# Last layer-0 down projection, its norm and the first value products, one stream after the other

## The chip, the cores and the metric

The kernel runs on one core of one Trainium2 chip. The metric is the device time of one execution in microseconds (us). TensorE (PE) multiplies matrices and loads its weights beside that (PEld); VectorE (DVE), ScalarE (ACT) and GpSimd (POOL) do the elementwise work; SyncE (SP) issues the loads.

## What is computed

Two layers of a backbone over two streams of 256 tokens with 2048 channels, latent (stream 0) and context (stream 1). Each layer is a mixer and a gated MLP, each behind an RMS norm with a shift and a scale that come from `c`. Layer 0 mixes by pooling, layer 1 by neighbourhood attention in which latent queries read the context keys and values too. In float32:

```
h  = h  + ml[:, 5] * conv_ffn(modulate(rms_norm(h,  norm2_g[0]), ...))    # latent, end of layer 0
hc = hc + mc[5]    * conv_ffn(modulate(rms_norm(hc, norm2_g[0]), ...))    # context
a_lat = modulate(rms_norm(h,  norm1_g[1]), ml[:, 0], ml[:, 1])            # start of layer 1
a_ctx = modulate(rms_norm(hc, norm1_g[1]), mc[0], mc[1])
q, k, v = a_lat @ w_qkv;  kc, vc = a_ctx @ w_qkv[:, D:]
def conv_ffn(u, ...): return (silu(conv3(u @ w_gate) + b) * (u @ w_up)) @ w_down    # 5504 hidden channels
def rms_norm(x, g):   return x * rsqrt(mean(x * x, channels) + 1e-6) * g
```

## The kernel before

Channels lie on the 128 partitions, so a stream is 16 tiles `h_of(s)[:, k, :]` of 128 x 256 (`hl` latent, `hc` context). Every float32 product is three products of split operands: a high half (rounded, float32r) and a low half (the rest), `hi*xh + hi*xl + lo*xh`. Weights are loaded from memory in pieces of up to 1024 columns into six staging rooms (`load`, `stage`); `split` makes the high half on ScalarE (line 143) and the low half on VectorE (line 145) in one of three `whp` buffers, or four while `extra` holds the pool `whx`.

The MLP's 43 hidden tiles are worked in chunks of four; the last chunk has three. `gate0` leaves a chunk's activations in `act` rooms (`act_tile`, seven of them) with both streams side by side, 512 columns. `down0` (lines 653 to 672) multiplies a chunk with its down weights: four groups `mg` of four output tiles, and for each output nine matmuls of 512 columns (three hidden tiles, lines 657 to 659) into a PSUM bank. In the last chunk VectorE adds the bank to `hl` and `hc` (line 663) and `n3.add` sums squares for the next norm: two squares on ScalarE (line 276), one add of 512 columns on VectorE (line 282). `pump` advances by one step what is left of layer 1's modulation at each call.

After the last output `n3.rstd()` works serially: matmuls of the square sums with ones (`n3s`, line 289), three small VectorE steps and a power on GpSimd (line 294), a diagonal (`n3d`, line 297), and a matmul that spreads the result over the partitions (`n3b`, line 299), left in PSUM. `normalise` (line 310 to 313) then makes, for each tile k and stream, y on VectorE, the high half of A on ScalarE and the low half on VectorE. y takes a `t2` tile, six of which exist. `_values` goes over four groups `kg` of four tiles k: it loads and splits a group of value weights, normalises the group for both streams, and does 48 matmuls of 512 columns into four banks `v_first` (two per stream; lines 869 to 871). The keys (`kq_tile`, line 934) come next.

Each engine works through its instructions in an order fixed before the run by a planner: it takes the earliest instruction in the program's text among those that it expects to be ready, and gives a tile any free buffer of its tag.

Of the kernel before, what the change touches and what calls it, by code (L numbers as in the profile page):

```python
# [10 lines left out]
F32 = mybir.dt.float32  # L11
F32R = mybir.dt.float32r
AF = mybir.ActivationFunctionType
ALU = mybir.AluOpType
# [3 lines left out]
P = 128  # L18
D = 2048
KT = D // P  # L20
T = 256
# [36 lines left out]
def kernel(ctx: ExitStack, tc: tile.TileContext, xT, cxT, wmod, wg, wu, wd, wp,  # L58
                         wq, wv, wo, vec, cc, rope, inv, strips, out):
    nc = tc.nc  # L60
# [94 lines left out]
    both = (0, 1)  # L155
# [105 lines left out]
    def M(l, which, k, s):  # L261
        return modT[l, which * 4 + k // 4][:, k % 4, s : s + 1]


    class Norm:


        def __init__(self, streams, pool, name):
            self.streams, self.pool, self.name = streams, pool, name
            self.n = T * len(streams)  # L270
            self.acc = None

        def add(self, h_of, k):
            sq = self.pool.tile([P, 512], F32, tag="t2", name=f"{self.name}q{k}")
            for s in self.streams:
                nc.scalar.activation(sq[:, T * s : T * s + T], h_of(s)[:, k, :], AF.Square)
            if k == KT - 1:
                self.last = sq
            elif self.acc is None:
                self.acc = sq  # L280
            else:
                nc.vector.tensor_tensor(self.acc[:, : self.n], self.acc[:, : self.n], sq[:, : self.n], op=ALU.add)

# [19 lines left out]

    def normalise(l, which, h_of, streams, rstd, pool, ks=range(KT), keep=A):

        for k in ks:
            a = ap0.tile([P, 2, 2, T], F32R, tag=f"A{k}", name=f"A{k}_{l}_{which}")
            y = pool.tile([P, 2, T], F32, tag="t2", name=f"nrm{l}{which}{k}")
            for s in streams:
                nc.vector.scalar_tensor_tensor(y[:, s], h_of(s)[:, k, :], M(l, which + 1, k, s),  # L310
                                               rstd[:, T * s : T * s + T], op0=ALU.mult, op1=ALU.mult)
# [4 lines left out]
            if l == 1 and k == 1:  # L316
                hold[:] = [ins.ins]
# [5 lines left out]
    with ExitStack() as ph0:  # L323
# [10 lines left out]
        def h_of(s):  # L334
            return hc if s else hl
# [50 lines left out]
        with ExitStack() as phs:  # L386
# [53 lines left out]
            def mixer(g):  # L440
# [3 lines left out]
                nc.sync.dma_start(inv_t, inv[:, g, :])  # L444
                gsc = st.tile([P, 8], F32, bufs=1, name=f"gsc{g}")
                gbi = st.tile([P, 8], F32, bufs=1, name=f"gbi{g}")
                pa = []
# [190 lines left out]

        n3 = Norm(both, f0, "n3")

        def down0(c, fs, acts, after=None):
            n = len(fs)
            last = c == len(chunks) - 1
            for mg in range(4):
# [4 lines left out]
                for m in range(4):  # L649
# [10 lines left out]
                    k = 4 * mg + m  # L660
                    if last:
                        for s in both:
                            nc.vector.scalar_tensor_tensor(h_of(s)[:, k, :], ps[:, T * s : T * s + T], M(0, 5, k, s),
                                                           h_of(s)[:, k, :], op0=ALU.mult, op1=ALU.add)
                        n3.add(h_of, k)
                    else:
                        y = f0.tile([P, 2, T], F32, tag="t2", name=f"dy{c}_{k}")
                        for s in both:
                            nc.scalar.activation(y[:, s], ps[:, T * s : T * s + T], AF.Copy, scale=M(0, 5, k, s))  # L669
                            nc.gpsimd.tensor_tensor(h_of(s)[:, k, :], h_of(s)[:, k, :], y[:, s], op=ALU.add)  # L670
                if after is not None:
                    after()

        r6 = late(NC)
# [24 lines left out]
        prev = (len(chunks) - 1, chunks[-1], [acts[f] for f in chunks[-1]])  # L699
        down0(*prev)  # L700
        for _ in pump:
            pass
        extra.clear()
        rooms.extend(-r for r in ring)

        rstd = n3.rstd()
        _values(bank, nc, ld, A, wv, 0, lambda ks: normalise(1, 0, h_of, both, rstd, f0, ks), v_first)
        hold.clear()

# [143 lines left out]

def _values(bank, nc, ld, A, wv, g, before, pv):

    pv.extend(bank("gu", f"v{g}_{i}") for i in range(4))
    for kg in range(4):
        parts = ld(wv[g, kg], f"wv{g}_{kg}")
        if before is not None:
            before(range(4 * kg, 4 * kg + 4))  # L860
        for i in range(4):
# [12 lines left out]
def _attention(tc, ap0, bank, ld, A, M, hl, wq, wv, wo, rope, strips, ident, v_first):  # L874
# [9 lines left out]
    with ExitStack() as es:  # L884
# [27 lines left out]
        def v_group(g):  # L912

            if g == 0:
                pv = v_first
            else:
                pv = []
                _values(bank, nc, ld, A, wv, g, None, pv)
# [293 lines left out]
```

## Time and profile before

| | us |
|---|---|
| median of 3 runs | 3107.48 |
| lowest and highest | 3105.3, 3110.52 |
| profiled execution | 3105.55 |
| its span, first to last instruction | 3103.8 |
| TensorE matmul busy | 3033.5 (98%) |
| VectorE, ScalarE, GpSimd busy | 1948.5, 1371.4, 820.2 |

The times are of whole executions; the profile is of one, and its rows count from the first instruction. A matmul's row gives when it starts and how long it takes through the array; matmuls overlap, so the distance between two starts is what one costs.

### The profile page before, as it was taken

Reading aid. Unit: us, or ns where it says so; the run is one execution under the profiler, and the core shown is the slowest. Engines: PE = TensorE matmul, PEld = TensorE weight load, DVE = VectorE, ACT = ScalarE, POOL = GpSimd, SP = SyncE. Lnnn points to the kernel's source line nnn. Section 1 sums busy time; section 2 is a strip of 40 time slices with the busy share of each in tenths; the row PEclk is TensorE's granted clock in tenths of the full one; section 3 lists DMA queues with packets and bytes.
Section 4 is the critical chain, followed back from the end, with each engine's and each line's share of the span. In section 5 each row is a group of like instructions: output and inputs, shape, how many; then the busy total and the mean of one; then the engine's idle time right before and its main releaser. Section 6 shows DMA issues by size and latency. Waiting matters only on the chain.

```text
span 3103.8 us, 40829 instructions
## 1 busy us (share of the span) xinstructions
PE 3033.5 (98%) x15082; PEld 2409.9 (78%) x15082; DVE 1948.5 (63%) x2748; ACT 1371.4 (44%) x2219; POOL 820.2 (26%) x823
## 2 busy tenths in 40 slices
PE   6999899999999999999999999999999999999998
PEld 2565558888888888888887787878778888888887
DVE  4445674384765748567485665474777677766676
ACT  4333455323233332333334444343545665656665
POOL 2011213213031130302213000000002466556665
PEclk9999999999999999999999999999999999999999
DMA  9888573274746648475573233332345565665563
GB/s 381 331 275 309 179 237 98 90 230 143 243 149 200 203 154 256 131 218 178 175 233 117 97 108 108 103 111 97 112 144 182 180 196 186 191 188 188 177 192 120
DMA packets 177927, 559.70 MB, mean 180 GB/s; under 512 B 17600, under 2 KB 22208, under 8 KB 177728
## 3 DMA queue, kind: packets, MB, share of 16 engines
q1 hardware_dynamic: 177728, 557.10, 55.6%
q8 instruction: 119, 1.95, 0.2%
q14 instruction: 80, 0.66, 0.1%
HBM read 554.93 MB, written 2.10 MB: 179 GB/s over the span
## 4 chain that ended last, share of the span: by engine, by line
PE 94%; DMA 2%; DVE 2%; POOL 1%; ACT 1%; issue 1%; SPq 0%; DVEq 0%; ACTq 0%; POOLq 0%
PE g L764 5%; PE u L764 5%; PE d L657 5%; PE d L659 5%; PE d L658 5%; PE d L809 4%; PE u L631 4%; PE u L632 4%; PE u L633 4%; PE g L631 4%; PE g L633 4%; PE g L632 4%; PE mod L193 3%; PE g L765 3%; PE u L765 3%; PE d L810 2%
## 5 line engine op out<-in xcount | busy, mean ns | idle before, releaser
L670 POOL TENSOR_TENSOR hl<-hl,dy 128x256 f32<-128x256 f32 x160 | 149.3, 933 | 957.9 <-ACT dy L669 956.6
L821 POOL TENSOR_TENSOR hl<-hl,dy 128x256 f32<-128x256 f32 x320 | 322.2, 1041 | 182.1 <-ACT dy L819 179.8
L241 DVE SCALAR_TENSOR_TENSOR macc<-wm,sc,macc 128x512 f32<-128x512 f32 (+1 forms) x360 | 325.0, 933 | 72.0 <-DMA wm<-wmod 71.2
L669 ACT ACTIVATE dy<-d,modT 128x256 f32<-128x256 f32 x320 | 133.4, 470 | 195.8 <-PE d L659 194.5
L193 PE MATMUL mod<-wm,sc 128*32 128x512 f32 x768 | 133.6, 619 | 23.7 <-DMA wm<-wmod 23.7
L670 POOL TENSOR_TENSOR hc<-hc,dy 128x256 f32<-128x256 f32 x160 | 127.0, 794 | 0.0
L145 DVE TENSOR_TENSOR wd_2l<-wd,wd_2h 128x1024 fp32r<-128x1024 f32 (+1 forms) x44 | 54.1, 1235 | 111.5 <-ACT wd_2h L143 111.5
L819 ACT ACTIVATE dy<-d,modT 128x512 f32<-128x512 f32 x160 | 104.5, 684 | 37.4 <-PE d L810 36.1
L908 POOL TENSOR_TENSOR rk<-rk,rp 128x256 f32<-128x256 f32 x16 | 13.8, 861 | 365.6 <-DVE rk L907 301.9
L145 DVE TENSOR_TENSOR wd_3l<-wd,wd_3h 128x1024 fp32r<-128x1024 f32 (+1 forms) x44 | 52.0, 1202 | 80.1 <-ACT wd_3h L143 80.1
L145 DVE TENSOR_TENSOR wd_1l<-wd,wd_1h 128x1024 fp32r<-128x1024 f32 (+1 forms) x44 | 53.5, 1221 | 58.4 <-ACT wd_1h L143 58.4
L466 POOL TENSOR_TENSOR pf<-ws,inv 128x256 f32<-128x256 f32 x32 | 27.7, 886 | 221.8 <-DVE ws L461 154.1
L193 PEld LDWEIGHTS mod<-wm,sc 128*32 128x32 f32 x768 | 23.5, 110 | 77.8 <-issue 60.3
L143 ACT CAST wd_1h<-wd 128x1024 fp32r<-128x1024 f32 (+1 forms) x44 | 45.3, 1031 | 79.4 <-PE u L632 50.7
L145 DVE TENSOR_TENSOR wd_0l<-wd,wd_0h 128x1024 fp32r<-128x1024 f32 (+1 forms) x44 | 53.3, 1220 | 39.5 <-ACT wd_0h L143 39.3
L994 ACT ACTIVATE sb<-sb,nm 128x512 f32<-128x512 f32 x64 | 46.2, 721 | 63.1 <-DVE nm L990 61.4
L143 ACT CAST wd_0h<-wd 128x1024 fp32r<-128x1024 f32 (+1 forms) x44 | 45.3, 1031 | 52.4 <-PE u L764 26.3
L657 PE MATMUL d<-act,wd_2h 128*128 128x512 f32 x172 | 68.0, 395 | 0.0
L657 PE MATMUL d<-act,wd_3h 128*128 128x512 f32 x172 | 67.9, 395 | 0.0
L658 PE MATMUL d<-act,wd_2h 128*128 128x512 f32 x172 | 67.9, 395 | 0.0
L657 PE MATMUL d<-act,wd_0h 128*128 128x512 f32 x172 | 67.9, 395 | 0.0
L658 PE MATMUL d<-act,wd_0h 128*128 128x512 f32 x172 | 67.9, 395 | 0.0
(1752 smaller groups left out, 9999.3 us busy)
## 6 DMA issues: line engine op xcount, KB each, us to landing
wm<-wmod SPq DMA_DIRECT2D x384, 512.0 KB, 6.1
wd<-wd SPq DMA_DIRECT2D x168, 512.0 KB, 4.3
wg<-wg SPq DMA_DIRECT2D x156, 512.0 KB, 4.6
wu<-wu SPq DMA_DIRECT2D x156, 512.0 KB, 4.5
wv<-wv SPq DMA_DIRECT2D x32, 512.0 KB, 3.8
wk<-wq SPq DMA_DIRECT2D x32, 512.0 KB, 3.9
wq<-wq SPq DMA_DIRECT2D x32, 512.0 KB, 3.8
wo<-wo SPq DMA_DIRECT2D x32, 512.0 KB, 3.9
```

Source lines behind the costliest of these rows:

```text
L145: eng.tensor_tensor(lo[:, :n], t[:, :n], hi[:, :n].bitcast(F32), op=ALU.subtract)
L193: nc.tensor.matmul(ps[32 * j : 32 * j + 32, :], sc[:, 4 * g + j, :], ts[j // 2][0][:, 512 * (j % 2) : 512 * (j % 2) + 512], start=(g == 0) ...
L241: nc.vector.scalar_tensor_tensor(acc[s], v, sc2[:, k, s : s + 1], acc[s], op0=ALU.mult, op1=ALU.add)
L631: nc.tensor.matmul(ps, hi[:, c : c + P], xh, start=(k == 0), stop=False)
L632: nc.tensor.matmul(ps, hi[:, c : c + P], xl, start=False, stop=False)
L633: nc.tensor.matmul(ps, lo[:, c : c + P], xh, start=False, stop=(k == KT - 1))
L657: nc.tensor.matmul(ps, hi[:, o : o + P], xh, start=(i == 0), stop=False)
L658: nc.tensor.matmul(ps, hi[:, o : o + P], xl, start=False, stop=False)
L670: nc.gpsimd.tensor_tensor(h_of(s)[:, k, :], h_of(s)[:, k, :], y[:, s], op=ALU.add)
L764: nc.tensor.matmul(ps, hi[:, c : c + P], flat(B[k]), start=(k == 0), stop=False)
L765: nc.tensor.matmul(ps[:, T:], lo[:, c : c + P], B[k][:, 0], start=False, stop=(k == KT - 1))
L821: nc.gpsimd.tensor_tensor(hl[:, k, :], hl[:, k, :], y[:, q], op=ALU.add)
```

## The change

- `down0` loses its last-chunk branch. A new `down0_last` works the last chunk in two halves of eight output tiles. In each half it loads and splits the weights of two groups, then does the eight outputs of the context stream and after them those of the latent one, with matmuls of 256 columns; evictions and square sums are per stream.
- There are two norms, one per stream. Their first square tile lies in `late_norm[0]` (room that layer 0's second norm no longer needs). Square sums of odd tiles are added on GpSimd, the others on VectorE. A stream's `rstd()` stands in the text right behind its eighth output of the second half.
- `values0` does the first value products by stream: groups 0 and 1 of the context stream, groups 0 and 1 of the latent one, then groups 2 and 3 with context ahead of latent. y lies in an `act` room. `extra.clear()` comes after it, so value weights have four hi/lo buffers.
- `gsc` and `gbi` of layer 0's mixer share two buffers each in place of four of their own.

```diff
     class Norm:
-        def __init__(self, streams, pool, name):
+        def __init__(self, streams, pool, name, room=None):
+            self.room = room
...
         def add(self, h_of, k):
-            sq = self.pool.tile([P, 512], F32, tag="t2", name=f"{self.name}q{k}")
-            for s in self.streams:
-                nc.scalar.activation(sq[:, T * s : T * s + T], h_of(s)[:, k, :], AF.Square)
+            if self.room is not None and self.acc is None:
+                sq = self.room
+            else:
+                sq = self.pool.tile([P, 512], F32, tag="t2", name=f"{self.name}q{k}")
+            for i, s in enumerate(self.streams):
+                nc.scalar.activation(sq[:, T * i : T * i + T], h_of(s)[:, k, :], AF.Square)
...
-                nc.vector.tensor_tensor(self.acc[:, : self.n], self.acc[:, : self.n], sq[:, : self.n], op=ALU.add)
+                eng = nc.gpsimd if self.room is not None and k % 2 else nc.vector
+                eng.tensor_tensor(self.acc[:, : self.n], self.acc[:, : self.n], sq[:, : self.n], op=ALU.add)
...
-    def normalise(l, which, h_of, streams, rstd, pool, ks=range(KT), keep=A):
+    def normalise(l, which, h_of, streams, rstd, pool, ks=range(KT), keep=A, more=False, room=None):
...
-            y = pool.tile([P, 2, T], F32, tag="t2", name=f"nrm{l}{which}{k}")
+            if room is None:
+                y = pool.tile([P, 2, T], F32, tag="t2", name=f"nrm{l}{which}{k}")
+            else:
+                y = room(f"nrm{l}{which}{k}_{streams[0]}", F32)[:, 0].rearrange("p (s t) -> p s t", s=2)
...
-                gsc = st.tile([P, 8], F32, bufs=1, name=f"gsc{g}")
-                gbi = st.tile([P, 8], F32, bufs=1, name=f"gbi{g}")
+                gsc = st.tile([P, 8], F32, tag="gsc", name=f"gsc{g}")
+                gbi = st.tile([P, 8], F32, tag="gbi", name=f"gbi{g}")
...
+        def down0_last(c, fs, acts):
+            n = len(fs)
+            norms = {s: Norm((s,), f0, f"n3{s}", late_norm[0][:, T * s : T * s + T]) for s in both}
+            res = {}
+            for half in range(2):
+                parts = [split(load(...), f"wd0_{c}_{mg}") for mg in (2 * half, 2 * half + 1)]
+                for s in (1, 0):
+                    for j in range(8):
+                        if j % 4 == 0:
+                            next(pump, None)
+                        k, m = 8 * half + j, j % 4
+                        ps = bank("d", f"d0_{c}_{k}_{s}")
+                        for i in range(n):
+                            hi, lo = parts[j // 4][i // 2]
+                            o = 512 * (i % 2) + P * m
+                            xh, xl = (x[:, T * s : T * s + T] for x in acts[i])
+                            nc.tensor.matmul(ps[:, :T], hi[:, o : o + P], xh, start=(i == 0), stop=False)
+                            nc.tensor.matmul(ps[:, :T], hi[:, o : o + P], xl, start=False, stop=False)
+                            nc.tensor.matmul(ps[:, :T], lo[:, o : o + P], xh, start=False, stop=(i == n - 1))
+                        nc.vector.scalar_tensor_tensor(h_of(s)[:, k, :], ps[:, :T], M(0, 5, k, s), h_of(s)[:, k, :],
+                                                       op0=ALU.mult, op1=ALU.add)
+                        norms[s].add(h_of, k)
+                    if half:
+                        res[s] = norms[s].rstd()
+            return res
+
+        def values0(rstd):
+            v_first.extend(bank("gu", f"v0_{i}") for i in range(4))
+            def part(kg, s, parts):
+                normalise(1, 0, h_of, (s,), rstd[s], f0, range(4 * kg, 4 * kg + 4), more=(s == 0), room=act_tile)
+                for o in range(2):
+                    for kk in range(4):
+                        ...
+            ws = []
+            for kg in range(2):
+                ws.append(ld(wv[0, kg], f"wv0_{kg}"))
+                part(kg, 1, ws[kg])
+            for kg in range(2):
+                part(kg, 0, ws[kg])
+            for kg in range(2, 4):
+                w = ld(wv[0, kg], f"wv0_{kg}")
+                for s in (1, 0):
+                    part(kg, s, w)
...
-        down0(*prev)
+        rstd = down0_last(*prev)
         for _ in pump:
             pass
+        rooms.extend(-r for r in ring)
+        values0(rstd)
         extra.clear()
-        rooms.extend(-r for r in ring)
-        rstd = n3.rstd()
-        _values(bank, nc, ld, A, wv, 0, lambda ks: normalise(1, 0, h_of, both, rstd, f0, ks), v_first)
```

## Rows read from the trace of the kernel before

**Rows 1.** The page: busy time of each engine.

```profile
PE 3033.5 (98%) x15082; PEld 2409.9 (78%) x15082; DVE 1948.5 (63%) x2748; ACT 1371.4 (44%) x2219; POOL 820.2 (26%) x823
```

**Rows 2.** Timeline of TensorE: start, length, line, operands; idle before in brackets.

```profile
1671.34 0.40 PE L657 MATMUL d<-act,wd_0h 128*128 128x512 f32 x1
...
1687.80 0.39 PE L659 MATMUL d<-act,wd_1l 128*128 128x512 f32 x1
...
1704.98 0.40 PE L659 MATMUL d<-act,wd_3l 128*128 128x512 f32 x1
...
1715.47 0.79 PE L869 MATMUL v<-wv_0h,A 128*128 128x512 f32 x1 [1.11 <-ACT A L312]
...
1720.11 0.39 PE L869 MATMUL v<-wv_0h,A 128*128 128x512 f32 x1
...
1761.62 0.39 PE L934 MATMUL k<-A,wk0h 128*128 128x512 f32 x1
```

**Rows 3.** The chain that ended last, in the hole: start, length, what.

```profile
1712.31 2.06 PE n3b L299 x2
...
1714.40 4.79 DVE nrm L310 x12
```

**Rows 4.** Windows around the hole, as its first line names them.

```profile
core 0: us, PE busy (x) PEld busy (x) DVE busy (x) ACT busy (x) POOL busy (x), PEclk, DMA share, GB/s
1705.40:1707.80 2.40, 0.00 (x0) 0.00 (x0) 2.25 (x5) 1.75 (x4) 0.00 (x0) 1.00 0.38 143
...
1709.80:1712.30 2.50, 0.00 (x0) 0.02 (x1) 1.20 (x6) 0.00 (x0) 1.02 (x1) 0.50 0.00 0
...
1720.10:1722.00 1.90, 1.90 (x10) 1.54 (x9) 1.90 (x4) 0.00 (x0) 0.00 (x0) 1.00 0.00 0
...
1715.00:1730.00 15.00, 14.14 (x53) 11.10 (x54) 15.00 (x37) 9.65 (x23) 0.00 (x0) 0.83 0.10 35
```

**Rows 5.** Layer 1's last down projection: its ends in the timeline; its weight loads.

```profile
3071.84 0.28 PE L805 MATMUL d<-actb,wd_0h 128*128 128x256 f32 x1
...
3089.00 0.28 PE L807 MATMUL d<-actb,wd_3l 128*128 128x256 f32 x1
...
L805 PEld LDWEIGHTS d<-actb,wd_3h x12: 192/192/192, 3084.7 to 3088.6; 128*128 128x128 f32 x12
```

**Rows 6.** The chain of the last norm, one stream alone, at the kernel's end.

```profile
3089.56 0.49 DVE hl L813
...
3090.55 1.07 PE n5s L289 x8
...
3093.36 1.23 PE n5b L299 x2
```

**Rows 7.** Lines on VectorE and GpSimd: min/median/max ns, first and last start.

```profile
L282 DVE TENSOR_TENSOR n5q<-n5q,n5q x14: 410/426/927, 3076.3 to 3090.1; 128x256 f32<-128x256 f32 x14
...
L145 DVE TENSOR_TENSOR wo15l<-wo,wo15h x2: 1218/1910/2601, 2348.6 to 2351.0; 128x1024 fp32r<-128x1024 f32 x2
...
L737 POOL TENSOR_TENSOR B<-nrmBz,B x8: 735/738/2947, 2364.5 to 2376.6; 128x256 fp32r<-128x256 f32 x8
```

**Rows 8.** Norm matmuls: timeline of TensorE, and the line of the broadcasts.

```profile
1707.81 1.95 PE L289 MATMUL n3s<-ones,n3q 128*128 128x1 f32 x16 [2.43 <-DVE n3q L282]
...
361.00 0.67 PE L299 MATMUL n2b<-n2d,ones 128*128 128x512 f32 x1 [0.53 <-DVE n2d L297]
...
L299 PE MATMUL n2b<-n2d,ones x2: 592/630/667, 361.0 to 361.5; 128*128 128x512 f32 x2
```

**Rows 9.** Timeline of ScalarE and VectorE: one weight group split; a value copied.

```profile
1679.06 1.55 ACT L143 CAST wd_2h<-wd 128x1024 fp32r<-128x1024 f32 x2
...
1680.69 1.82 DVE L145 TENSOR_TENSOR wd_2l<-wd,wd_2h 128x1024 fp32r<-128x1024 f32 x2
...
1754.11 0.59 ACT L921 COPY vt<-v 128x512 f32<-128x512 f32 x1 [2.12 <-PE v L871]
```

**Rows 10.** The page's loads: KB each, median us from issue to landing.

```profile
wv<-wv SPq DMA_DIRECT2D x32, 512.0 KB, 3.8
```

More of the change, by code (lines that the diff above doesn't have):

```diff
@@ L302 @@
     A = {}
-    def normalise(l, which, h_of, streams, rstd, pool, ks=range(KT), keep=A):
+    def normalise(l, which, h_of, streams, rstd, pool, ks=range(KT), keep=A, more=False, room=None):
         for k in ks:
-            a = ap0.tile([P, 2, 2, T], F32R, tag=f"A{k}", name=f"A{k}_{l}_{which}")
-            y = pool.tile([P, 2, T], F32, tag="t2", name=f"nrm{l}{which}{k}")
-            for s in streams:
+            if more:
+                a = keep[k]
+            else:
+                a = ap0.tile([P, 2, 2, T], F32R, tag=f"A{k}", name=f"A{k}_{l}_{which}")
+            if room is None:
+                y = pool.tile([P, 2, T], F32, tag="t2", name=f"nrm{l}{which}{k}")
+            else:
+                y = room(f"nrm{l}{which}{k}_{streams[0]}", F32)[:, 0].rearrange("p (s t) -> p s t", s=2)
+            for i, s in enumerate(streams):
                 nc.vector.scalar_tensor_tensor(y[:, s], h_of(s)[:, k, :], M(l, which + 1, k, s),
-                                               rstd[:, T * s : T * s + T], op0=ALU.mult, op1=ALU.mult)
+                                               rstd[:, T * i : T * i + T], op0=ALU.mult, op1=ALU.mult)
                 nc.scalar.activation(a[:, 0, s, :], y[:, s], AF.Identity, bias=M(l, which, k, s))
@@ L315, in normalise @@
             keep[k] = a
-            if l == 1 and k == 1:
+            if l == 1 and k == 1 and not more:
                 hold[:] = [ins.ins]
@@ L637, in gu0 @@
             return res
-        n3 = Norm(both, f0, "n3")
         def down0(c, fs, acts, after=None):
             n = len(fs)
-            last = c == len(chunks) - 1
             for mg in range(4):
@@ L660, in down0 @@
                     k = 4 * mg + m
[L661 to L670, printed above, removed]
+                    y = f0.tile([P, 2, T], F32, tag="t2", name=f"dy{c}_{k}")
@@ L671, in down0 @@
+                    for s in both:
+                        nc.scalar.activation(y[:, s], ps[:, T * s : T * s + T], AF.Copy, scale=M(0, 5, k, s))
+                        nc.gpsimd.tensor_tensor(h_of(s)[:, k, :], h_of(s)[:, k, :], y[:, s], op=ALU.add)
                 if after is not None:
                     after()
+        def down0_last(c, fs, acts):
[3 more added lines that the diff above has]
+            for half in range(2):
+                parts = [split(load(lambda a, b: wd[0, mg, :, fs[0] + a // 512 : fs[0] + b // 512, :], 512 * n, f"wd0_{c}_{mg}"),
+                               f"wd0_{c}_{mg}") for mg in (2 * half, 2 * half + 1)]
+                for s in (1, 0):
[17 more added lines that the diff above has]
+            return res
@@ new lines, in values0 @@
+        def values0(rstd):
[4 more added lines that the diff above has]
+                    for kk in range(4):
+                        k = 4 * kg + kk
+                        hi, lo = parts[kk // 2]
+                        w = 512 * (kk % 2)
+                        xh, xl = (A[k][:, q, s, P * o : P * o + P] for q in range(2))
+                        ps = v_first[2 * s + o]
+                        nc.tensor.matmul(ps, xh, hi[:, w : w + 512], start=(k == 0), stop=False)
+                        nc.tensor.matmul(ps, xh, lo[:, w : w + 512], start=False, stop=False)
+                        nc.tensor.matmul(ps, xl, hi[:, w : w + 512], start=False, stop=(k == KT - 1))
+            ws = []
[8 more added lines that the diff above has]
+                    part(kg, s, w)
@@ L851, with _values @@
             nc.sync.dma_start(out[:, a:b, :], hl[:, a:b, :])
-def _values(bank, nc, ld, A, wv, g, before, pv):
+def _values(bank, nc, ld, A, wv, g, pv):
     pv.extend(bank("gu", f"v{g}_{i}") for i in range(4))
@@ L858, in _values @@
         parts = ld(wv[g, kg], f"wv{g}_{kg}")
-        if before is not None:
-            before(range(4 * kg, 4 * kg + 4))
         for i in range(4):
@@ L917, in v_group @@
                 pv = []
-                _values(bank, nc, ld, A, wv, g, None, pv)
+                _values(bank, nc, ld, A, wv, g, pv)
             v = at.tile([P, 4, 512], F32, tag="v", name=f"vt{g}")
```

## The prediction

> **What bounds the kernel now.** I read the page first: TensorE is busy for 98% of the span [rows 1]. So only what TensorE waits for, or what runs on it at the lower clock, can be won; work of the other engines counts where TensorE waits for it. Next I looked for the change's own stretch, from the first matmul of the last layer-0 down projection (1671.34) to the first key matmul (1761.62), which is 90.28 us [rows 2]. The reader is to see one hole in it. The last down matmul starts at 1704.98 and the matmuls follow each other at 0.23 us, so the work ends at 1705.21; the first value product starts at 1715.47. That hole is 10.26 us. In it stands a serial chain over both streams: last evictions and square sums on VectorE, the ones-matmuls n3s (1.95 us), the power on GpSimd, the broadcast n3b (2.06), then twelve normalising products on VectorE, 4.79 us, before the first low half of A [rows 3, 8]. The windows show what the hole does to the clock: 1.00 while TensorE stands still in 1705.4 to 1707.8, 0.50 from 1709.8, and 1.00 again only from 1720.1 [rows 4]. 0.50 is the 1.2 GHz level. Nine value matmuls lie between 1715.47 and 1720.11, 4.64 us. The other 183 of the 192 take 1720.11 to 1761.62, or 0.2268 each, so nine at that pace would take 2.04 us; 2.60 us is lost there. After that TensorE does not wait up to the keys. So 10.26 + 2.60 = 12.86 us of the stretch are not product work at full pace, and of it the norm's own matmuls must stay in some form.
>
> **The change part by part.** *Down projection by stream.* 144 matmuls of 512 columns become 288 of 256, each with its own weight load. The old part takes 1705.21 - 1671.34 = 33.87 us. Its first 72 start between 1671.34 and 1687.80, 71 steps of 0.2318 [rows 2]; 144 x 0.2318 = 33.38, and the other 0.49 is for two small pairs of modulation matmuls in the second half, which stay. For 256 columns the same pattern stands in layer 1's last down projection: 144 matmuls from 3071.84 to 3089.00, a pitch of 0.120 [rows 5]. 288 x 0.120 = 34.56. So the split costs 1.18 us.
>
> The rows show that a weight load of 0.19 us goes under the matmul before it, since the pitch is 0.120 [rows 5]. The Trainium skill, "TensorE: Matmul & The Clock Gate", section "The mechanism", says that weight loads overlap running matmuls only when the row group differs. By that rule all 144 added loads would stand open; the trace of this kernel does not agree, so it is a rival with a small chance only.
>
> *Norm per stream.* Two groups of eight ones-matmuls instead of sixteen: one such group took 1.07 us [rows 6]. The broadcast of 512 columns amid full-clock work in layer 0, n2b, came in two pieces that start 0.5 apart, the last 0.59 long [rows 8]: 1.1 us, so 0.55 for 256. Together 2 x 1.6 = 3.2 us, now on TensorE's path but no longer in a hole.
>
> *Values.* The same 192 matmuls: 192 x 0.2268 = 43.55 us.
>
> Sum without any wait: 34.56 + 0.49 + 3.20 + 43.55 = 81.80 us, against 90.28: 8.48 us is the most that can be won.
>
> *What covers the chains.* One stream's chain is shown at the kernel's end: from the last eviction at 3089.56 to the end of the broadcast, 3093.36 + 1.23 = 3094.59, 5.0 us [rows 6]. The context chain has the latent block of the second half over it: 72 x 0.120 = 8.64 us. The latent chain has the context values of two groups over it: 48 x 0.2268 = 10.9 us. Both covers are longer than 5.0, if VectorE serves the chain promptly. If the cover is gone, a chain costs its 5.0 us and some 2.6 us of low clock.
>
> *VectorE behind it.* Back to back, its 256-wide products cost 0.40 us each (twelve in 4.79 [rows 3]); a low half of a 1024-wide weight piece costs 1.2, and a 256-wide square sum 0.42 [rows 7]. From the last context matmul to the last latent one are 8.64 + 1.60 = 10.2 us. In them VectorE has nine evictions (3.6), four square sums (1.7; the odd ones go to GpSimd), the chain's small steps (0.9) and the two low halves of the first value weights (2.4): 8.6 us. These weight halves cannot come earlier: the four hi/lo buffers hold the second half's down weights until the latent block has gone through its first four outputs, while before, the same low halves were made under the down projection. 1.6 us are left, four of the eight products (3.2 us) that the first context value group wants. So these end up to 1.6 us after TensorE would like them; with matmuls of tiles that are ready going first I take 1.2. Afterwards a part of 24 matmuls lasts 5.44 us and asks VectorE for eight products and one low half, 4.4 us: VectorE gains ground, so no further wait is put down.
>
> *TensorE's own queue.* The ones-matmuls and broadcasts are put among other matmuls in an order fixed beforehand, and wait there if the other engines are later than planned. The one case amid running work is n2b, with 0.53 us idle before it; with nothing to fill in, n3s waited 2.43 [rows 8]. Our case is nearest to n2b, so 0.53 x 2 = 1.1 us; bounds 0 and 4.9.
>
> *Half turn.* The second half's weights wait for buffers that come free 4.3 us (36 x 0.120) before they are due; casts of 1.55 and low halves of 1.82 follow in a row [rows 9], 3.4 us. Nothing is put down; 0 to 1 us.
>
> *POOL adds.* GpSimd does seven of the fourteen square sums per stream, 0.74 each alone. The slowest one beside VectorE's low halves took 2.95, and a low half beside a GpSimd one took 2.60 instead of 1.22 [rows 7]. The Trainium skill, "SBUF — State Buffer", section "Who interferes with whom", calls the shared port pair an exclusive lock; the two durations fit it. One such collision adds 2.2 us to a chain that has 3.6 us (context) or 5.9 us (latent) of slack: nothing, unless two come together.
>
> *Loads.* The same eight down pieces and eight value pieces in the same order on SP's queue, nothing new before them. A value piece lands 3.8 us after its issue [rows 10]; the first two need staging rooms that come free about when the second half begins, 17 us (144 x 0.120) before they are due: 0.
>
> *Rooms, tags.* y takes activation rooms, of which there are seven and four are free before the down projection ends, enough for one group: 0. Shared gsc/gbi tags, one more weight buffer for the values: 0. Afterwards the first key matmul needs one value bank copied out; before, that copy (0.59 us) ran at 1754.11 [rows 9]; now the context banks end 5.4 us ahead of the keys. Price 0; without that lead 0.6 plus a handover.
>
> Sum: 81.8 + 1.2 + 1.1 = 84.1 us, 6.2 less than 90.28. The profiled execution took 3105.55 (its span 3103.8), 1.9 below the median of 3107.48; I take the saving from the median: 3101.3.
>
> **Rivals.** *Paced by VectorE.* The first two or three value parts wait, chains late, 3.5 to 8 us of idle in pieces no longer than the 2.4 us that left the clock at 1.00 [rows 4]: with 5.5 of idle, 90.28 - 81.8 - 5.5 leaves 3.0 us, 3104.5. For it: VectorE was busy without a break from 1715 to 1730 already [rows 4], and its 8.6 of 10.2 us leave nothing for a slip. Against: after 1720.11 the 183 matmuls came at an even 0.2268 all the same [rows 2].
>
> *No wait at all.* 8.5 less: 3099.0.
>
> *Chains stand open (slower).* If the ones-matmuls of a stream stand in TensorE's queue ahead of the matmuls meant to cover them, as they do in the program's text for the context stream, each chain costs 5.0 + 0.6 of eviction and 2.6 of low clock: 2 x 8.2 = 16.4 us. 81.8 + 16.4 - 90.28 = 7.9 slower: 3115.4. It decides once waits pass 8.5 us. Against it: n2b was placed amid running matmuls with 0.53 us lost [rows 8].
>
> *Weight loads stand open.* 144 more loads of 0.19 us [rows 5] add 27.4 us; less the 6.2 won elsewhere it is 21.2 slower: 3128.7. The pitch of 0.120 speaks against it [rows 5].
>
> **How the numbers follow.** About 0.2%, 6.2 us, is what a measurement can tell from no change. Forecast (waits of 1 to 3.5 us, so 5.0 to 7.5 won): 0.54; no wait or under 1 us: 0.18; paced: 0.21; chains open: 0.06; weight loads: 0.01. The forecast's middle lies on the bound, so half of its chance counts as faster: 0.27 + 0.18 = 0.45. Slower: 0.06 + 0.01 = 0.07. Within: 0.27 + 0.21 = 0.48. The range runs from no wait, less 1.5 for the spread of the runs shown (3105.3 to 3110.52), 3097.5, to the point where waits eat it all, 3107.5; about 0.12 lies outside, mostly the slower rivals.
>
> **What would show it.** Right: down matmuls at 0.120 pitch, a granted clock of 1.00 from 1671 to the keys, idle of TensorE under 3.5 us in all, the first key matmul about 84 us after the first down matmul. Wrong: idle before the ones-matmuls or broadcasts over 1 us; value matmuls waiting for low halves of A or of wv; clock at 0.50 anywhere there; a stretch elsewhere that changed.

## The result and the profile after

| | before | after |
|---|---|---|
| median, us (15 runs each, same chip) | 3108.2 | 3112.88 |
| lowest and highest | 3104.23, 3110.92 | 3109.36, 3117.74 |
| ratio after to before, 95% interval | | 1.0019 [1.0012, 1.0026] |
| span of the profiled execution | 3103.8 | 3111.3 |
| first down matmul to first key matmul | 90.28 | 95.72 |

The change made the kernel 0.19% slower, where the forecast was 3101.3 us and the range ended at 3107.5. The profiled span grew by 7.5 us: 5.44 in the stretch, 2.16 ahead of it, and 0.1 less behind it. The 2.16 lies within the scatter of single executions: kernels below whose text is the same up to there begin the stretch anywhere from 1670.46 to 1677.17.

The page's line of busy times answers to [rows 1]; TensorE's share is the same, GpSimd has 12 us more.

```profile
PE 3038.1 (98%) x15228; PEld 2418.3 (78%) x15228; DVE 1946.6 (63%) x2750; ACT 1372.7 (44%) x2219; POOL 832.2 (27%) x838
```

TensorE's timeline after, which answers to [rows 2] and [rows 3] (L696 to L698 down, L295 ones-matmuls, L305 broadcasts, L719 to L721 values, L990 keys; n31 is the context norm, n30 the latent one):

```profile
1673.50 0.28 PE L696 MATMUL d<-act,wd_0h 128*128 128x256 f32 x1
...
1692.49 0.40 PE L165 MATMUL modt_23s<-modr,quad 128*128 128x16 f32 x2 [1.43 <-DVE hl L699]
...
1696.02 0.36 PE L696 MATMUL d<-act,wd_2h 128*128 128x256 f32 x1 [0.67 <-DVE modT L181]
...
1703.60 0.39 PE L696 MATMUL d<-act,wd_2h 128*128 128x256 f32 x1 [0.58 <-DVE hc L699]
...
1704.78 0.50 PE L295 MATMUL n31s<-ones,n2acc 128*128 128x1 f32 x4
...
1707.86 0.48 PE L305 MATMUL n31b<-n31d,ones 128*128 128x256 f32 x1 [0.97 <-DVE n31d L303]
...
1713.45 0.63 PE L719 MATMUL v<-wv_0h,A 128*128 128x512 f32 x2
1714.58 0.39 PE L696 MATMUL d<-act,wd_3h 128*128 128x256 f32 x1 [0.50 <-DVE hl L699]
...
1719.52 0.28 PE L698 MATMUL d<-act,wd_3l 128*128 128x256 f32 x1
...
1727.90 0.50 PE L295 MATMUL n30s<-ones,n2acc 128*128 128x1 f32 x4
...
1730.62 0.70 PE L305 MATMUL n30b<-n30d,ones 128*128 128x256 f32 x2 [1.76 <-DVE n30d L303]
1732.43 0.50 PE L719 MATMUL v<-wv_0h,A 128*128 128x512 f32 x1 [1.11 <-ACT A L324]
...
1734.64 0.79 PE L721 MATMUL v<-wv_0h,A 128*128 128x512 f32 x1 [0.64 <-DVE A L325]
...
1739.90 0.39 PE L721 MATMUL v<-wv_0h,A 128*128 128x512 f32 x1
...
1769.22 0.39 PE L990 MATMUL k<-A,wk0h 128*128 128x512 f32 x1
```

The hole of 10.26 us [rows 3] is gone. Small waits stand in its place from the half turn on, and one larger group behind 1727.90: the latent chain, open. The reader should look at where 1727.90 lies: the latent down work ended at 1719.52, the ones-matmuls that follow from it ran 8.4 us later, and nothing was left to run beside what comes after them. The windows show the rest of the price:

```profile
core 0: us, PE busy (x) PEld busy (x) DVE busy (x) ACT busy (x) POOL busy (x), PEclk, DMA share, GB/s
1690.00:1700.00 10.00, 7.69 (x58) 7.00 (x58) 9.62 (x25) 4.23 (x10) 2.73 (x4) 1.00 0.53 173
...
1704.70:1719.60 14.90, 13.17 (x90) 11.57 (x89) 12.70 (x30) 7.59 (x17) 2.29 (x3) 1.00 0.15 43
1710.00:1720.00 10.00, 9.24 (x58) 7.85 (x58) 10.00 (x22) 7.10 (x16) 1.59 (x2) 1.00 0.26 73
1720.00:1730.00 10.00, 8.67 (x42) 6.86 (x40) 4.47 (x8) 1.99 (x4) 1.40 (x2) 1.00 0.40 139
...
1732.40:1739.90 7.50, 6.83 (x16) 4.90 (x17) 7.50 (x20) 5.00 (x12) 0.00 (x0) 0.54 0.00 0
```

VectorE is full at the half turn (9.62 of 10) and in the later part of the latent block (10.00 of 10; 12.70 of 14.90 in the whole block), then half idle (4.47 of 10) while the latent chain waits its turn. Behind the chain the granted clock is 0.54, mostly the 1.2 GHz level, as behind the old hole [rows 4]. VectorE's timeline says what it was full of:

```profile
1686.88 1.29 DVE L251 STREAM_TRANSPOSE modu<-macc 128x512 f32<-128x512 f32 x2
1688.10 1.18 DVE L145 TENSOR_TENSOR wd_2l<-wd,wd_2h 128x1024 fp32r<-128x1024 f32 x1
...
1689.93 0.68 DVE L252 TENSOR_REDUCE modr<-modu 128x16 f32<-128x512 f32 x1
1690.53 0.92 DVE L145 TENSOR_TENSOR wd_2l<-wd,wd_2h 128x512 fp32r<-128x512 f32 x1
1691.37 0.68 DVE L252 TENSOR_REDUCE modr<-modu 128x16 f32<-128x512 f32 x1
1691.96 1.25 DVE L699 SCALAR_TENSOR_TENSOR hl<-d,modT,hl 128x256 f32<-128x256 f32 x3
...
1693.81 1.69 DVE L145 TENSOR_TENSOR wd_3l<-wd,wd_3h 128x1024 fp32r<-128x1024 f32 x1
...
1721.02 2.78 DVE L145 TENSOR_TENSOR wv_1l<-wv,wv_1h 128x1024 fp32r<-128x1024 f32 x2
1723.72 0.41 DVE L288 TENSOR_TENSOR n2acc<-n2acc,n30q 128x256 f32<-128x256 f32 x1
1728.89 0.16 DVE L298 TENSOR_REDUCE n30v<-n30s 128x2 f32<-128x4 f32 x1 [4.76 <-PE n30s L295]
```

At the half turn the end of the modulation (L251, L252) and the two low halves of `wd_2` stand ahead of latent evictions (1691.96, three in a row, late), and TensorE waits 1.43 us for the bank; the two low halves of `wd_3` follow from 1693.81. For the latent norm the last sum is done at 1724.1, 4.6 us behind the last down matmul, because the low halves of `wv_1` went first; but TensorE asks for it only at 1727.90, and VectorE then idles 4.76 us.

From the starts in this timeline the stretch divides as follows. Product work is counted at 0.120 us for a down and 0.2268 for a value matmul, as in the forecast; the excess includes the forecast's 3.2 us of norm and 0.49 us of modulation matmuls.

| part | us | down, values | excess |
|---|---|---|---|
| first half, to the modulation's matmuls | 17.16 | 144, 0 | -0.12 |
| half turn, to n31s | 14.12 | 81, 0 | 4.40 |
| n31s to n31b | 3.08 | 9, 0 | 2.00 |
| n31b to last down | 11.66 | 53, 14 | 2.12 |
| last down to n30s | 8.38 | 1, 34 | 0.55 |
| n30s to n30b | 2.72 | 0, 0 | 2.72 |
| n30b to first key | 38.60 | 0, 144 | 5.94 |

The broadcasts count to the part that begins with them. The excesses make 17.61; less 3.69 it is 13.92 us of waits and low clock, where 2.3 were forecast: 81.80 + 13.92 = 95.72.

### The profile page after: what moved, and what is told of

The parts are those of the page before. It is cut to its first block, busy times and chain, and to the rows that moved or that the text cites. A ratio compares the mean times of both kernels' runs of the same rounds, so it can differ in the third digit from the quotient of the medians.

```text
span 3111.3 us, 41143 instructions
## 1 busy us (share of the span) xinstructions
PE 3038.1 (98%) x15228; PEld 2418.3 (78%) x15228; DVE 1946.6 (63%) x2750; ACT 1372.7 (44%) x2219; POOL 832.2 (27%) x838
## 4 chain that ended last, share of the span: by engine, by line
PE 94%; DVE 2%; DMA 2%; POOL 1%; ACT 1%; issue 1%; SPq 0%; DVEq 0%; ACTq 0%; POOLq 0%
PE g L822 5%; PE u L822 5%; PE d L666 5%; PE d L668 5%; PE d L667 5%; PE d L867 4%; PE u L643 4%; PE u L644 4%; PE u L645 4%; PE g L643 4%; PE g L645 4%; PE g L644 4%; PE mod L193 3%; PE g L823 3%; PE u L823 3%; PE d L868 2%
## 5 line engine op out<-in xcount | busy, mean ns | idle before, releaser
L145 DVE TENSOR_TENSOR wd_3l<-wd,wd_3h 128x1024 fp32r<-128x1024 f32 (+1 forms) x44 | 52.5, 1213 | 80.2 <-ACT wd_3h L143 80.2
L667 PE MATMUL d<-act,wd_2h 128*128 128x512 f32 x160 | 63.2, 395 | 0.0
L666 PE MATMUL d<-act,wd_0h 128*128 128x512 f32 x160 | 63.2, 395 | 0.0
L668 PE MATMUL d<-act,wd_2l 128*128 128x512 f32 x160 | 63.2, 395 | 0.0
L667 PE MATMUL d<-act,wd_0h 128*128 128x512 f32 x160 | 63.1, 395 | 0.0
```

Of the source, the lines that this page charges most:

```text
L145: eng.tensor_tensor(lo[:, :n], t[:, :n], hi[:, :n].bitcast(F32), op=ALU.subtract)
L666: nc.tensor.matmul(ps, hi[:, o : o + P], xh, start=(i == 0), stop=False)
L667: nc.tensor.matmul(ps, hi[:, o : o + P], xl, start=False, stop=False)
L668: nc.tensor.matmul(ps, lo[:, o : o + P], xh, start=False, stop=(i == n - 1))
```

## The experiments

All edits are to the changed kernel. "Stretch" is first down to first key matmul in the profiled execution. Ratios are to the kernel before on the same chip.

| run | stretch | median | ratio, 95% |
|---|---|---|---|
| e1_groups_in_turn | 92.36 | 3110.11 | 1.0008 [0.9998, 1.0017] |
| e2_values_only | 90.61 | 3108.26 | 1.0002 [0.9992, 1.0012] |
| e3_no_lat_chain | 88.70 | 3106.43 | 0.9996 [0.9986, 1.0005] |
| e4_mod_first | 92.78 | 3118.34 | 1.0031 [1.0018, 1.0044] |
| e5_sums_between | 95.00 | 3112.41 | 1.0016 [1.0007, 1.0025] |
| e6_pump_early | 95.08 | 3111.79 | 1.0014 [1.0005, 1.0024] |
| e7_both | 95.98 | 3115.01 | 1.0023 [1.0013, 1.0033] |
| e8_sums_vector | 94.96 | 3113.05 | 1.0018 [1.0009, 1.0027] |
| e10_quarters | 93.03 | 3110.94 | 1.0010 [1.0001, 1.0019] |
| e11_no_vlow | 93.52 | 3112.79 | 1.0016 [1.0007, 1.0025] |
| e12_no_vlow_between | 92.11 | 3111.19 | 1.0014 [1.0005, 1.0023] |
| e13_quarters_between | 94.66 | 3111.30 | 1.0012 [1.0004, 1.0021] |
| e14_down_first | 95.64 | 3115.32 | 1.0026 [1.0015, 1.0037] |
| e15_order | 92.54 | 3110.41 | 1.0010 [1.0002, 1.0019] |
| e16_order_quarters | 89.69 | 3108.37 | 0.9999 [0.9990, 1.0008] |
| e17_quarters_no_lat | 86.88 | 3104.26 | 0.9985 [0.9976, 0.9994] |

**Which part costs.** e1 takes the value groups in turn, context then latent in each:

```diff
-            for kg in range(2): ... part(kg, 1, ws[kg])
-            for kg in range(2): part(kg, 0, ws[kg])
-            for kg in range(2, 4):
+            for kg in range(4):
```

> The first value products go group by group, context part then latent part (one context part of 24 matmuls, 5.4 us, ahead of the first latent one in place of two). The stretch from the first matmul of the last down projection to the first key matmul is 90.28 us before and 95.72 us after. Theory 1 (the latent norm chain stands open because VectorE delivers the latent square sums late; the context values that should cover it are used up before): with half the cover the hole before the first latent value product does not shrink, the stretch is 95 to 100 us, ratio to before 1.001 to 1.004. Rival (the order of the groups itself, its held weight buffers and late low halves, costs the time): the stretch falls to 88 to 91 us, ratio 0.998 to 1.001.

Only 24 context value matmuls are then left to cover the latent chain, and yet the stretch is 3.36 us shorter, between the two ranges expected. Its TensorE timeline:

```profile
1718.60 0.50 PE L295 MATMUL n30s<-ones,n2acc 128*128 128x1 f32 x4
...
1721.31 0.70 PE L305 MATMUL n30b<-n30d,ones 128*128 128x256 f32 x2 [1.76 <-DVE n30d L303]
1723.12 0.67 PE L719 MATMUL v<-wv_0h,A 128*128 128x512 f32 x1 [1.11 <-ACT A L324]
```

The two waits are the same 1.76 and 1.11: the chain stands open here too, and the 24 further matmuls that were to cover it in the changed kernel covered nothing. The low clock lasted only to about 1726.6, 3.5 us in place of 7.5, and 2.06 of the 3.36 us lie behind the broadcast (excess 3.88, against 5.94). So the amount of cover decided nothing here; whether the place of the chain's matmuls does is tested with e15 below.

e2 keeps the values by stream, with the down projection and one norm for both streams as before:

```diff
-            norms = {s: Norm((s,), f0, f"n3{s}", ...) for s in both}
+            n3 = Norm(both, f0, "n3")
+            ...  # four groups, matmuls of 512 columns
+            pb = n3.rstd()
+            return {s: pb[:, T * s : T * s + T] for s in both}
```

> Down projection and norm of both streams together as before, first value products by stream as after. Theory 1: the hole of before (10 us) is back, nothing of the latent chain stands apart; the stretch is 89 to 92 us, ratio 0.999 to 1.001. Rival (the stream order of the values costs the time, not the down projection and its chains): stretch 94 us or more, ratio 1.001 to 1.003.

90.61 and no measurable difference: the value order by itself is free within the measurement; the loss comes with the down projection and norms by stream. e3 normalises the latent stream with the context's factor, so that the latent chain is left out:

```diff
-                    if half:
+                    if half and s == 1:
                         res[s] = norms[s].rstd()
+            res[0] = res[1]
```

> The latent stream is normalised with the context stream's factor, so the latent chain from the square sums to the broadcast is left out (the output is not the reference's); all else as after. Theory 1: the latent value products follow without a hole and at full clock; the stretch falls by 7 to 10 us to 86 to 89 us, ratio to before 0.998 to 0.9995. Rival (half turn, 256-column matmuls and late low halves cost the time; the chain is a small part): it falls by under 4 us, stretch over 92 us, ratio over 1.000.

7.02 us shorter, with no low clock. That is the latent chain's price in place, 1.6 us of it the forecast's own norm matmuls. 88.70 is still 8.5 over the forecast's work without them (80.2), so the chain is not all.

**The half turn.** e4 ends the modulation ahead of the projection, e6 calls its last steps in the first half, e10 works the first half in two quarters, which frees two of the four hi/lo buffers 8.6 us (72 matmuls) earlier:

```diff
 e4:
+        for _ in pump: pass
         rstd = down0_last(*prev)
-        for _ in pump: pass
 e6:
-                        if j % 4 == 0:
+                        if half == 0 and (j % 2 == 0 if s else j % 4 == 0):
                             next(pump, None)
 e10:
-                for s in (1, 0):
-                    for j in range(8):
+                for s, j in [(s, j) for a in ((range(4), range(4, 8)) if half == 0 else (range(8),)) for s in (1, 0) for j in a]:
```

> What is left of layer 1's modulation is finished ahead of the last down projection; all else as after. At the half turn TensorE of after steps 1.83, 0.48 and 0.95 us around the modulation's small matmuls, some 2.5 us more than matmuls at pitch. Theory 1: those 2.5 us go and about as much is lost where the modulation now stands by itself, or the latent hole takes it; the stretch is 92 to 95.5 us and the time within 3 us of after. Rival (the half turn is the cause of the loss): the stretch falls to 90 us or less and the time is that of before or better.

> As after, but the last five steps of the modulation are called in the first half of the down projection (every second context output, then the latent ones), not at the half turn. Theory 2 (at the half turn VectorE has the modulation's transposes and sums, the low halves of four weight pieces and the evictions at once, so that banks come free late): the steps of 1.83, 0.48 and 0.95 us there shrink to pitch, the stretch falls by 2 to 3 us to 93 to 94 us, with the latent hole as it was; ratio 1.0005 to 1.0020. Rival (the low halves alone are late): under 1 us is won.

> First half in two quarters (group 0 context then latent, group 1 context then latent), so two hi/lo buffers come free 8.6 us earlier and the second half's four low halves need not be made in a row; second half as in the changed kernel. Theory that the half turn is a price of holding four hi/lo buffers for a whole half: the steps of 1.83, 0.97 and 0.86 us around the half turn shrink to under 0.5, stretch 95.7 less about 2.5 to 3 = 93, median 3110. Rival that the half turn is the end of the modulation alone (its transposes and sums come there in any case): steps stay, stretch 95 to 96, median 3113. The latent hole (broadcast step 2.3, clock 0.50) stays in both.

e4's waits at the half turn went, 2.94 us less in the stretch, but the stretch began at 1679.19 and the kernel was the slowest of all, 5.5 us over the changed one where 3 were expected at most: the modulation's work on VectorE now stood open ahead of the stretch.

```profile
1678.97 0.37 PE L165 MATMUL modt_22s<-modr,quad 128*128 128x16 f32 x2 [3.57 <-DVE modr L252]
```

Behind this wait the granted clock was 0.54 from 1679.2 to 1682.9, inside the stretch. e6 moved the waits (0.96 for the modulation at 1683.52, then 1.56 for an eviction at 1698.58) and won 0.6, as its rival had it. e10 won 2.69: 1.70 at the half turn (excess 4.40 to 2.70), 0.14 before it and 0.86 behind the latent broadcast. That last part takes from 37.56 us (e4) to 38.60 (the changed kernel) in the kernels with this order of matmuls, so the 0.86 is not shown to come from the edit. e10's TensorE timeline, against 1692.49 and 1696.02 above:

```profile
1690.46 0.37 PE L165 MATMUL modt_23s<-modr,quad 128*128 128x16 f32 x2
...
1695.42 0.36 PE L695 MATMUL d<-act,wd_2h 128*128 128x256 f32 x1 [1.09 <-DVE modT L181]
```

The wait of 1.43 is gone: with buffers free earlier, the low halves no longer stand in a row with the modulation's end. The other, 0.67 before and 1.09 now, stays; `wd_3`'s low halves still come there.

**Is VectorE late, or is TensorE's order wrong?** e5 puts the latent ones-matmuls between the two context value parts, e7 is e5 and e6 together, e8 adds all square sums on VectorE:

```diff
 e5:
+                        with ExitStack() as behind:
+                            if kg == 1 and s == 1:
+                                behind.enter_context(tc.issue_after(sums[0]))   # last latent ones-matmul
 e8:
-                eng = nc.gpsimd if self.room is not None and k % 2 else nc.vector
+                eng = nc.vector
```

> As after, but the context products of the second value group are issued behind the latent stream's ones-matmuls, so that these stand in TensorE's queue between the two context parts and not behind both. Theory 1a (the latent chain stands open because its ones-matmuls come in TensorE's queue after the work that should cover the chain; their data were there 3.8 us earlier): the hole of 4.2 us between them and the first latent product shrinks to under 1 us, the clock stays at 1.00, and the stretch (90.28 us before, 95.72 after, 88.70 without the chain) is 89 to 92 us; ratio to before 0.9990 to 1.0010. Rival 1b (the data come late, VectorE being full): TensorE waits as long ahead of the ones-matmuls instead, stretch 94 us or more.

> Both edits, the ones-matmuls between the context parts and the early modulation. If the two causes are separate the gains add: stretch 86.5 to 89 us, ratio to before 0.9980 to 0.9995, faster than both kernels. If one wait only gives way to another (VectorE full from the half turn to the latent products), the stretch is 90 us or more and the ratio 0.9995 to 1.0015.

> As after, but all square sums are added on VectorE and none on GpSimd. Theory 1 gives GpSimd's sums no part in the loss: seven more sums per stream on VectorE, 0.4 us each, make it later: stretch 95.5 to 98 us, ratio 1.0015 to 1.0030. Rival (the hand-overs between VectorE and GpSimd in the running sum hold up the latent chain): stretch 93 us or less.

e8 left the holes as they were (1.75 and 1.11), so GpSimd's sums do not open the chain. In e5 the wait changed its place:

```profile
1721.67 0.61 PE L295 MATMUL n30s<-ones,n2acc 128*128 128x1 f32 x4 [2.11 <-DVE n2acc L288]
...
1731.05 0.50 PE L725 MATMUL v<-wv_0h,A 128*128 128x512 f32 x1 [0.65 <-ACT A L324]
...
1733.25 0.50 PE L727 MATMUL v<-wv_0h,A 128*128 128x512 f32 x1 [1.01 <-DVE A L325]
```

It looked as if VectorE were late whatever the order, and e7, where the gains did not add (95.98), fitted that. e11 and e12 tested it: the low halves of the first two groups of value weights, 5.2 us of VectorE, are left out, and those products take the high half in their place; e12 has e5's order as well. e13 is e5's order with the quarters, nothing left out.

```diff
-                ws.append(ld(wv[0, kg], f"wv0_{kg}"))
+                ws.append(ld(wv[0, kg], f"wv0_{kg}", low=False))
```

> The low halves of the first two groups of value weights are not made (5.2 us of VectorE in the latent block; the products take the high half in their place, so the values are rounded). Theory that VectorE is late for the latent sums: the last square sum is done about 2.5 to 3 us earlier, the stretch falls by 2 to 3.5 us to 92 to 93.5, if the planned order puts the latent ones-matmuls earlier too; 95 if they stay behind the second context part. Rival that the chain of one stream is simply longer than its cover: stretch stays at 95 to 96.

> The same low halves left out, and the latent ones-matmuls put between the two context value parts. Theory that VectorE is late: the 2.11 us that TensorE waited for the latent square sum in that place fall to under 0.5, and with the chain begun 3 us earlier the steps at the first latent values (1.05 and 1.40) fall to under 1 in sum: stretch 95.0 less 3.5 = 91.5, median 3108.5, no clock of 0.50. Rival (order and chain length): the wait before the ones-matmuls goes, those behind the broadcast stay, stretch 93 to 94.

> Quarters in the first half and the latent ones-matmuls between the context value parts; the whole computation is done. Theory of a shared VectorE: the half turn's gain comes (2.5 to 3 us), the wait before the ones-matmuls stays at 2 us or less, stretch 91.5 to 92.5, median 3109 to 3110, not under the kernel before. Rival that gains do not add, as with the earlier two edits together: 94 to 95, median 3112.

The theory came out only in part. e11 won 2.2 us and its median nothing that can be measured. e13 came out as its rival had it: the half turn gave 1.71, the wait at the ones-matmuls stayed at 2.12, and the clock fell behind it and again at the first latent values. In e12 the wait at the ones-matmuls should have fallen under 0.5 and was 1.52, and 1.11 and 1.01 stood at the first latent values. VectorE's timeline of e12 shows why:

```profile
1718.42 0.48 DVE L700 SCALAR_TENSOR_TENSOR hl<-d,modT,hl 128x256 f32<-128x256 f32 x1 [2.13 <-PE d L699]
1719.48 0.48 DVE L700 SCALAR_TENSOR_TENSOR hl<-d,modT,hl 128x256 f32<-128x256 f32 x1 [0.58 <-PE d L699]
```

VectorE, with less to do, now waited 2.13 us for TensorE: all 24 matmuls of the first context part (14 in the changed kernel) had been put ahead of the last latent down matmul. So the cover was partly spent before the chain could begin; and in every one of these kernels the broadcast stood behind all or nearly all of the other 24 (46 to 48 values ahead of it), so that nothing covered what follows it.

e14 puts the values behind the last latent down matmul; e15 adds the ones-matmuls behind 24 and the broadcast behind 36 of the context values; e16 is e15 with the quarters; e17 is the quarters with e3's edit, which leaves the latent chain out.

```diff
+                            if kg == 0 and s == 1:
+                                behind.enter_context(tc.issue_after(sums[0]))               # last down matmul; e14, e15, e16
+                            if kg == 1 and s == 1:
+                                behind.enter_context(tc.issue_after(sums[2 if o else 1]))   # broadcast, ones; e15, e16
```

> All context value matmuls stand behind the last latent down matmul in TensorE's queue; nothing else is set by hand. Order theory (14 value matmuls were spent before the latent outputs were through): alone it wins little, since the ones-matmuls stay behind most of the 48 context value matmuls and the broadcast right behind them: stretch 95.7 less 0 to 1.5. VectorE theory: the latent outputs wait for banks, the stretch grows by 1 to 2 us to 97.

> As the last one, and the latent ones-matmuls stand behind 24 context value matmuls, the broadcast behind 36, the other 12 behind the broadcast. Order theory: the chain is covered; the waits at the ones-matmuls, at the broadcast and at the first latent values fall from 3.5 us and the nine to fourteen half-clock matmuls to under 1.5 us in sum: stretch 95.7 less 4.5 to 6 = 90 to 91, median 3107 to 3108. VectorE theory: the waits appear at the ones-matmuls (2 us) and at the broadcast (1 us or more) as in the two earlier runs with a set place: stretch 94 to 96.

> The set order and the quarters together; the whole computation is done. Order theory: gains add, 95.7 - 2.7 - 5 = 88, which is 2.3 us under the kernel before: median 3105.5. VectorE theory: 93 to 94.5, median 3110 to 3112.

> Quarters, and the latent stream normalised with the context's factor (the latent sums, their chain and 1.3 us of its matmuls are left out). If the half turn's 2.7 us and the latent chain's 7.0 are separate, the stretch is 95.7 - 9.7 = 86, median 3103.5. If one wait hides the other it stays at 88 to 89, median 3106.

e14 won nothing in the stretch, as the order theory had it; e15 won 3.18 and e16 6.03, 1.5 and 1.7 us short of what that theory expected. TensorE's timeline of e16:

```profile
1710.88 0.39 PE L695 MATMUL d<-act,wd_3h 128*128 128x256 f32 x1 [0.79 <-DVE hl L698]
...
1712.80 0.39 PE L695 MATMUL d<-act,wd_3h 128*128 128x256 f32 x1 [0.58 <-DVE hl L698]
...
1713.85 0.28 PE L697 MATMUL d<-act,wd_3l 128*128 128x256 f32 x1
...
1720.77 0.60 PE L295 MATMUL n30s<-ones,n2acc 128*128 128x1 f32 x4 [1.19 <-DVE n2acc L288]
...
1724.56 0.59 PE L305 MATMUL n30b<-n30d,ones 128*128 128x256 f32 x2
...
1727.76 0.40 PE L726 MATMUL v<-wv_0h,A 128*128 128x512 f32 x1
...
1760.77 0.39 PE L997 MATMUL k<-A,wk0h 128*128 128x512 f32 x1
```

No wait at the broadcast and none at the first latent value (1727.76), in e15 neither: the order did it, with all of VectorE's work in place. From n30s to the keys the excess without the norm matmuls is 7.1 us in the changed kernel, 1.9 in e15 and 0.3 in e16. What VectorE owes is the 1.19 at the ones-matmuls and the bank waits in the latent block (0.79 and 0.58). The excess of that block, 3.90 from n31b to the last down matmul against 2.12 with 14 values put between, is more than these: e16's clock was at the lower level there for 3.4 us, as the last section shows. e17 at 86.88, 8.84 less than the changed kernel, says that the half turn and the latent chain are separate: the full sum is 9.7, and the missing 0.87 is about what e10 won behind the latent broadcast, which e17 does not have. In medians e16 (ratio up to 1.0008) is clear of the changed kernel (from 1.0012), and e15 (up to 1.0019) is not. e16 ties with the kernel before; no kernel that does the whole computation beat that one.

## Why the prediction was wrong

- **Down projection by stream** was right. The first half's 144 matmuls took 17.16 us, 0.119 each. The rule of the Trainium skill, "TensorE: Matmul & The Clock Gate", section "The mechanism", by which the added weight loads would stand open, is not borne out by this trace either. The same section also lets a load into the background weight buffer go ahead; no run here shows which buffer a load takes.
- **"Half turn: nothing is put down; 0 to 1 us"** failed: 3.9 us (4.40 less 0.49). The step costed casts and low halves in a row, 3.4 us within 4.3, but not what else VectorE has there: the modulation's transposes and sums (1.29 for two, then twice 0.68, then the small adds) and the evictions, in one queue. e10 shows that the late buffers were 1.7 of it; the rest is read from the timeline, for e4 and e6 moved the modulation's waits and did not remove them.
- **"What covers the chains"**: for the context chain nearly right: 2.00 us from n31s to n31b, less the forecast's 1.07 for ones-matmuls, leaves 0.9, the wait of 0.97 at its broadcast. For the latent chain wrong, and this is the step that turned the sign. 48 matmuls of 10.9 us were counted as cover from the last latent matmul on; 14 ran before it and 34 before the ones-matmuls, and none behind them. The part from n30s to the keys has 8.66 us of excess, 7.1 without the norm matmuls, where 0.53 was put down under **TensorE's own queue**. The rows of n2b that 0.53 came from [rows 8] say what one broadcast waited, not that an order fixed beforehand keeps a cover for its sums and for the first products behind it.
- **"VectorE behind it"**: 1.2 us put down; 2.1 measured, 1.57 in the latent block (2.12 less the broadcast's 0.55) and 0.55 up to n30s. The ledger's share, 8.6 of 10.2 us, was about right (12.70 of 14.90), but the free time came early and from 1710 VectorE was full, and a full queue also delays evictions, so banks (the wait of 0.50 at 1714.58), which the ledger let pass.
- **The rival "chains stand open"** had the mechanism but only 0.06 of the chance, and it took both chains or none. Its 8.2 us per chain counts 1.6 of norm matmuls that 81.8 has already, and its 2.6 of low clock holds a wait of 0.39 (1719.64 in the kernel before); without the double count it is 6.6 per chain and 3112.2 us for both. That this is near the measured 3112.88 is luck: one chain open (7.1), the other's wait (0.9), the half turn (3.9) and VectorE (2.1) make 14.0, past the 8.5 at which it decides.
- **The clock**, forecast at 1.00 throughout, went to 0.54 for 7.5 us. The paced rival took pauses of up to 2.4 us as harmless [rows 4]; here it fell behind waits of 1.76 and 1.11.

What stays open: how the last 7.9 us of e16 over 81.8 could be won (six waits on VectorE, 5.2 us, remain), and why e7 and e14 have medians over 3115 with a stretch like that of the changed kernel. In e14's profile 4.7 us more lie behind the first key matmul (3116.9 - 1770.11, against 3111.3 - 1769.22), but this part, whose text is the same in all, takes from 1340.4 us (e5) to 1346.8 in the profiles, and 1346.3 in e16: one profile does not tell a cause.

## What to carry to other kernels

Work that is ready in time covers a chain only if the queue's fixed order puts it beside each of the chain's steps: count, for every matmul of the chain, how many independent ones stand between it and the next, not how many there are in all. Before giving a stream its own pass, list all that shares the engine which evicts (here VectorE: end of modulation, low halves, evictions, sums), since holding buffers for a longer pass pushes such work together. When a wait moves and does not shrink on an edit, try the edits in one set: e5 alone won 0.7 us, with the broadcast's place and the values' it was 3.2, with the buffers 6.0 (a fall of the clock stands in each of these profiles).

## What the hardware showed

Equal waits had different effects on the clock. The broadcast of the context norm waited 0.97 us in all sixteen kernels that have the norms by stream, behind the same nine down matmuls. Right behind it the granted clock fell to the lower level in five profiles (e5, e8, e11, e14, e16) and stayed at 1.00 in the other eleven. Windows of 3.4 us behind that broadcast, first e16, then e15:

```profile
1703.90:1707.30 3.40, 3.40 (x17) 3.30 (x16) 2.50 (x7) 1.97 (x5) 0.00 (x0) 0.51 0.00 0
```

```profile
1705.30:1708.70 3.40, 3.39 (x27) 3.16 (x26) 2.99 (x8) 2.36 (x6) 0.00 (x0) 1.00 0.00 0
```

At the latent ones-matmuls it was the other way round: e15 waited 1.15 us and fell, e16 waited 1.19 and did not. The windows of 3.6 us that begin 2.1 us after those waits, first e15, then e16:

```profile
1723.70:1727.30 3.60, 3.60 (x11) 2.82 (x9) 0.48 (x2) 0.00 (x0) 0.13 (x1) 0.53 0.06 24
```

```profile
1722.90:1726.50 3.60, 3.60 (x17) 2.95 (x16) 1.80 (x6) 0.80 (x2) 0.11 (x1) 1.00 0.06 24
```

The first was mostly at the lower level and did 11 matmuls, the second 17. From n30s to the keys e15 took 41.57 us and e16 40.00; these 1.57 us are about what the fall cost. In the latent block, where the other fall lies, e16 took 0.56 longer than e15 though its bank waits were shorter (1.37 us, against 1.80). So each of these two stretches holds a fall of the clock, and the 2.85 between them is not the quarters' work alone. e13, after a wait of 2.12, fell too (0.55 from 1722.9 to 1726.7), and e12, after 1.52, did not. A wait of about a microsecond thus sometimes costs its length again, and a difference of 1.5 us between two such profiles may be the clock alone.
